# Making the last tile ahead of a norm in two halves of the tokens

## The chip, the cores and the metric

The kernel runs on one core of a Trainium2 chip. Its engines work side by side, each through its own queue in order: TensorE (PE; its weight loads are listed as PEld), VectorE (DVE), ScalarE (ACT), GpSimd (POOL) and SyncE (SP), which issues transfers. The metric is the device time of one execution in microseconds, the median over several runs.

## The reference

Two layers of a transformer-like trunk over 256 context tokens and 256 image tokens of width 1024. The context is needed as keys and values only in layer 1, so layer 0 works on 512 tokens and layer 1, after its keys and values, on 256. What matters here is how each half of a layer ends:

```python
def rms_norm(x, w):
    xf = x.astype(jnp.float32)
    y = xf * lax.rsqrt(jnp.mean(xf * xf, axis=-1, keepdims=True) + RMS_EPS)
    return (y * w.astype(jnp.float32)).astype(x.dtype)
...
    x = x + g1 * parallel_mixers(p, attn, lp)        # ends in merged @ w_out
    x = x + g2 * swiglu(modulate(x, norm2_w[l], sh2, s2), ffn_w_gate[l], ffn_w_up[l], ffn_w_down[l])
return rms_norm(x, final_norm_w)
```

A norm needs the sum of squares over all 1024 features of a token, so nothing after it can start until the last feature tile of `x` is there.

## The kernel before

Activations lie with features on the 128 partitions and tokens on the free axis: `x` is 8 tiles of 128 x 512, of which layer 1 uses the right 256 columns. Float32 products are made of three fp32r products: each operand is split into a high part and a rest (`whi`, `wlo`, `hh`, `hl`), and `mm3` (lines 209 to 211) issues high x high, high x rest and rest x high into one PSUM accumulation.

Weights arrive as units of 128 x 1024 in `raw`; ScalarE casts them to `whi` (line 171), VectorE subtracts to get `wlo` (line 174). There are five buffers for `raw` and four each for `whi` and `wlo`, so the cast of a unit waits until the unit four before it is used up.

Four places in the program have the same shape: 8 output tiles `j` are made one after another, each of 24 products (w_out, k = 0..7) or 33 (w_dn, second half of the FFN, k = 0..10), and the last one is followed by a norm.

- A: w_out of layer 0, then norm 2, then the first FFN products (`k_major`, PSUM tiles `pmk`)
- B: w_dn of layer 0, then norm 1 of layer 1, then `wide_gen` (`pmw`)
- C: w_out of layer 1, then norm 2 and `k_major`
- D: w_dn of layer 1, then the final norm and the output

After each tile `residual` adds it to `x` on VectorE; `sumsq_add` squares `x[j]` on ScalarE and adds the square to `acc` on VectorE. Around the last tile `sums_of` multiplies `acc`, and then the last square, with a column of ones on TensorE (PSUM tile `pmss`): the sums over the partitions, one column for every 128 tokens. `rstd` scales and adds epsilon on VectorE (`rs`) and takes the power -1/2 on GpSimd. `rstd_bcast` makes a diagonal matrix of it on VectorE (`dg`) and multiplies it with ones on TensorE, which gives the factor on all partitions (`psrb`). `norm_tiles` then makes `nt`, `nh`, `hh` and `hl` of the 8 tiles on VectorE and ScalarE.

While this chain runs, TensorE is given other work: filters of the next layer (`pspf`), spectra (`pssp`), and modulation matmuls (`psmod`, `chunk_mods`). At the end (D), `x` is weighted (`xw`, ScalarE), transposed on TensorE into `psfin`, scaled by the factor into `fin`, and written out by four transfers of 256 KB.

The order on each engine comes from the order of the code and a scheduler that moves instructions by its own estimate; `tc.keep_in_program_order` holds an instruction at its place. On the chip each queue is in order: an instruction that waits holds all that stand behind it.

Of the kernel before, what the change touches and what calls it, by code (L numbers as in the profile page):

```python
# [14 lines left out]
AF = mybir.ActivationFunctionType  # L15
# [3 lines left out]
P = 128  # L19
D = 1024  # L20
# [82 lines left out]
def trunk_kernel(ctx: ExitStack, tc: tile.TileContext, I, out: bass.AP):  # L103
# [32 lines left out]
    def load_const(name, shape):  # L136
        t = const(name, shape)
        SY.dma_start(out=t, in_=I[name])
        return t

    def split(hi, lo, src):
        S.copy(hi, src)
        V.tensor_sub(lo, src, f32(hi))
# [63 lines left out]

    def mm3(o, wh, wl, xh, xl, first, last):
        T.matmul(o, lhsT=wh, rhs=xh, start=first, stop=False)  # L209
        T.matmul(o, lhsT=wh, rhs=xl, start=False, stop=False)  # L210
        T.matmul(o, lhsT=wl, rhs=xh, start=False, stop=last)  # L211

# [14 lines left out]
    ones = const("ones", [P, P])  # L227
    V.memset(ones, 1.0)
    halfexp = const("halfexp", [P, 8])
    V.memset(halfexp, -0.5)  # L230
# [51 lines left out]
    def chunk_mods(n):  # L282
        for _ in range(min(n, len(chunks))):
            c, kt, raw = chunks.popleft()
            if kt == 0:
                mod_bank[c] = side("mod")
            o = mod_bank[c]
            for q in range(4):
                T.matmul(
                    o[32 * q : 32 * q + 32, :P], lhsT=csf[:, kt, :], rhs=raw[:, q * P : q * P + P],  # L290
                    start=(kt == 0), stop=(kt == KT - 1),
                )
            if kt == KT - 1:
                chunk_tail(c)
# [28 lines left out]

    def last_sq(x, c0, c1):
        sq = t2(s="sq")
        S.activation(sq[:, c0:c1], x[KT - 1][:, c0:c1], AF.Square)
        return sq

    def sums_of(o, v, c0, c1, first, last):

        nt = (c1 - c0) // P
        for t in range(nt):
            sl = slice(c0 + t * P, c0 + t * P + P)
            T.matmul(
                o[:, t : t + 1], lhsT=v[:, sl], rhs=ones[:, 0:1],
                start=first and t == 0, stop=last and t == nt - 1,
            )
# [10 lines left out]
    def rstd_bcast(r2, c0, c1):  # L348

        nt = (c1 - c0) // P  # L350
# [7 lines left out]
        )  # L358
        rb = side("rb")
        T.matmul(rb[:, c0:c1], lhsT=ones, rhs=dg[:, : c1 - c0], start=True, stop=True)  # L360
        return rb

# [97 lines left out]
    def filter_mm(l, p, o):  # L460
        w3, _, f = flt[l]
        f[p, o] = side("pf")
        T.matmul(f[p, o], lhsT=hk[:, p * P : p * P + P], rhs=w3[o], start=True, stop=True)

# [184 lines left out]
    r2 = rstd(o, 0, NTOK)  # L649
    rb = rstd_bcast(r2, 0, NTOK)  # L650
    chunk_mods(KT)
# [3 lines left out]
    for l in range(DEPTH):  # L655
# [28 lines left out]
        if l == 0:  # L684
# [5 lines left out]
            for g in range(4):  # L690
# [11 lines left out]
                os_ = next(w0)  # L702
            start.close()
        else:
            for i, h in enumerate(norm_tiles(l, 0, x, rb, 0, NTOK, range(KT))):
# [533 lines left out]
        def residual(o, j, gi):  # L1239
            for k in halves:  # L1240
# [3 lines left out]
                )  # L1244

        if l == 0:
# [3 lines left out]
        for j in range(KT):  # L1250
# [4 lines left out]
            if j == KT - 1:  # L1255
                so = bank("ss")
                sums_of(so, acc, C0, NTOK, True, False)
                if full:
                    filter_mm(1, 0, 0)
            residual(o, j, 2)  # L1260
            if j < KT - 1:
                sumsq_add(x, acc, j, C0, NTOK)
# [4 lines left out]
        sums_of(so, last_sq(x, C0, NTOK), C0, NTOK, False, True)  # L1267
        r2 = rstd(so, C0, NTOK)
# [4 lines left out]
        if full:  # L1273
            filter_mm(1, 1, 0)
        chunk_mods(BUB[1])

# [4 lines left out]
        if full:  # L1281
            for po in ((0, 0), (0, 1), (1, 0)):
                filter_keep(1, *po)
            filter_mm(1, 1, 1)
            filter_keep(1, 1, 1)
        acc = t2(s="acc")
        xw, fin = {}, {}

        def final_weigh(j):
            xw[j] = t2(s="xw")  # L1290
            S.activation(xw[j][:, CS], x[j][:, CS], AF.Copy, scale=nw[:, 2 * DEPTH, j : j + 1])

        def final_turn(j):

            for t in range(NX // P):
                if j % 4 == 0:
# [4 lines left out]
        for half in range(2):  # L1301
# [18 lines left out]
            for j in range(KT):  # L1320
                o = bank("d")
                for k in range(NFH):
                    n = j * NFH + k
                    if n % 8 == 0:
                        hi, lo = unit("w_dn", l, half, n // 8)
                    c = (n % 8) * P
                    mm3(
                        o[:, CS], hi[:, c : c + P], lo[:, c : c + P],
                        hid[k][0][:, CS], hid[k][1][:, CS], k == 0, k == NFH - 1,
                    )  # L1330
                    if n % 8 == 7:
                        done()
                if half == 1 and j == KT - 1:
                    for _ in sg_:
                        pass
                    so = bank("ss")
                    sums_of(so, acc, C0, NTOK, True, False)
                    if full:
                        parts, fwd, nyq, skip = flt[1]
                        spectrum_mm(1, "B0", parts, fwd, nyq)  # L1340
                residual(o, j, 5)
                if half == 1 and j < KT - 1:
                    sumsq_add(x, acc, j, C0, NTOK)
                if not full and half == 1:
                    if j:
                        final_turn(j - 1)
                    if j < KT - 1:
                        final_weigh(j)
                next(sg_, None)
        sums_of(so, last_sq(x, C0, NTOK), C0, NTOK, False, True)  # L1350
        r2 = rstd(so, C0, NTOK)
        if full:
            spectrum_out(1, "B0", skip)
            spectrum_mm(1, "B1", parts, fwd, nyq)
            spectrum_out(1, "B1", skip)
            spectrum_mm(1, "A0", parts, fwd, nyq)
            rb = rstd_bcast(r2, C0, NTOK)
            spectrum_mm(1, "A1", parts, fwd, nyq)
            spectrum_mm(1, "C0", parts, fwd, nyq)


    final_weigh(KT - 1)
    final_turn(KT - 1)
    for t in range(NX // P):
        for h in range(2):
            y = t2(s="fin")
            if h:
                S.activation(y, fin[t, h], AF.Copy, scale=r2[:, t : t + 1])
            else:
                V.tensor_scalar(y, fin[t, h], r2[:, t : t + 1], None, op0=ALU.mult)  # L1370
            SY.dma_start(out=out[t * P : t * P + P, h * 512 : h * 512 + 512], in_=y)

# [154 lines left out]
```

## Time and profile before

| | us |
|---|---|
| median of 3 runs (1328.41 to 1329.69) | 1329.41 |
| profiled execution | 1328.54 |
| its span, first to last instruction | 1326.0 |
| TensorE busy (matmul) | 1292.9 |
| VectorE busy | 935.6 |
| ScalarE busy | 608.6 |

A timeline row gives the start in us from the span's start, the duration in us, the engine, the source line, the operation, out<-in tiles, their shape (for a matmul 128*128 is the weight and 128x512 the moving operand), and how many were merged; in brackets how long the engine had been idle, and what released it. A matmul's duration is a latency: in a row of products the distance of two starts is what one costs.

### The profile page before, as it was taken

The page shows a single profiled execution, that of the slowest core. Times are in us where ns is not written, and L with a number is a line of the kernel's source. Part 1 is how long each engine was busy: PE and PEld are TensorE (multiplying, and loading weights), DVE is VectorE, ACT ScalarE, POOL GpSimd, SP SyncE. Part 2 cuts the span into 40 slices and gives each one's busy share as a digit, 9 for nine tenths or more (in the row PEclk, how much of TensorE's full clock was granted, in tenths as well). Part 3 has the DMA queues.
Part 4 walks back from the last instruction along what each step waited for, and adds up shares of the span by engine and source line. Part 5 has one row for each costly group of instructions (what it writes and reads, how often), then busy time and mean ns, then how long its engine had stood idle before and what let it go on. Part 6 is the DMA issues. An engine that isn't in the chain of part 4 may idle for free.

```text
span 1326.0 us, 19996 instructions
## 1 busy us (share of the span) xinstructions
PE 1292.9 (98%) x7714; PEld 1128.2 (85%) x7714; DVE 935.6 (71%) x1599; ACT 608.6 (46%) x1060; POOL 61.9 (5%) x69
## 2 busy tenths in 40 slices
PE   4999999999999999999999999999999999999997
PEld 3778788888888887888888888889989999999997
DVE  3687788798987356666667767966889876655554
ACT  3564333367753246222222224365468854543443
POOL 0000500300000000000000000001210000000000
PEclk7999999999999999999999999999999999999999
DMA  9532334343245552554555554424434457455551
GB/s 343 210 127 77 104 104 143 126 143 112 93 157 160 174 209 73 173 164 159 174 174 175 182 168 143 159 80 128 134 110 139 151 192 247 159 179 188 179 187 49
DMA packets 68063, 203.85 MB, mean 154 GB/s; under 512 B 7552, under 2 KB 13824, under 8 KB 67968
## 3 DMA queue, kind: packets, MB, share of 16 engines
q1 hardware_dynamic: 67968, 202.58, 46.1%
q8 instruction: 60, 0.98, 0.3%
q14 instruction: 35, 0.29, 0.1%
HBM read 201.50 MB, written 1.05 MB: 153 GB/s over the span
## 4 chain that ended last, share of the span: by engine, by line
PE 75%; issue 16%; DVE 5%; ACT 2%; POOL 1%; DMA 0%; DVEq 0%; POOLq 0%; ACTq 0%
PE pmn L209 14%; PE pmn L211 14%; PE pmn L210 14%; PE pmd L209 3%; PE pmd L210 3%; PE pmd L211 3%; PE pmb L209 2%; PE pmb L210 2%; PE pmb L211 2%; PE pmw L676 2%; PE pmw L678 2%; PE pmw L677 2%; PE psav L1188 1%; PE pspt L1166 1%; DVE wlo L174 1%
## 5 line engine op out<-in xcount | busy, mean ns | idle before, releaser
L171 ACT CAST whi<-raw 128x1024 fp32r<-128x1024 f32 (+2 forms) x312 | 288.1, 929 | 470.8 <-PE pmn L210 214.4
L209 PE MATMUL pmn<-hh,whi 128*128 128x512 f32 (+1 forms) x1328 | 449.9, 339 | 0.3 <-DVE vst L721 0.3
L210 PE MATMUL pmn<-hl,whi 128*128 128x512 f32 (+1 forms) x1328 | 448.1, 337 | 0.0
L211 PE MATMUL pmn<-hh,wlo 128*128 128x512 f32 (+1 forms) x1328 | 447.7, 337 | 0.3 <-DVE wlo L174 0.3
L174 DVE TENSOR_TENSOR wlo<-raw,whi 128x1024 fp32r<-128x1024 f32 (+2 forms) x312 | 335.7, 1078 | 143.3 <-ACT whi L171 141.0
L211 PEld LDWEIGHTS pmn<-hh,wlo 128*128 128x128 f32 x1328 | 252.0, 190 | 27.7 <-issue 1.1
L209 PEld LDWEIGHTS pmn<-hh,whi 128*128 128x128 f32 x1328 | 252.1, 190 | 27.6 <-issue 0.9
L210 PEld LDWEIGHTS pmn<-hl,whi 128*128 128x128 f32 x1328 | 252.1, 190 | 26.0 <-issue 0.7
L259 DVE CUSTOM_DVE_ANT_0 junk<-raw,cb,pack_a 128x1024 bf16<-128x1024 f32 x144 | 187.0, 1299 | 1.4
L209 PE MATMUL pmd<-hh,whi 128*128 128x512 f32 (+1 forms) x352 | 119.2, 339 | 0.0
L210 PE MATMUL pmd<-hl,whi 128*128 128x512 f32 (+1 forms) x352 | 118.7, 337 | 0.0
L211 PE MATMUL pmd<-hh,wlo 128*128 128x512 f32 (+1 forms) x352 | 118.0, 336 | 0.0
L210 PEld LDWEIGHTS pmd<-hl,whi 128*128 128x128 f32 x352 | 66.8, 190 | 7.2 <-issue 0.5
L211 PEld LDWEIGHTS pmd<-hh,wlo 128*128 128x128 f32 x352 | 66.8, 190 | 7.1 <-issue 0.2
L209 PEld LDWEIGHTS pmd<-hh,whi 128*128 128x128 f32 x352 | 66.8, 190 | 7.1 <-issue 0.2
L1314 DVE TENSOR_TENSOR sg<-sg,pmn 128x512 f32<-128x512 f32 (+1 forms) x42 | 23.3, 554 | 65.0 <-PE pmn L211 65.0
L345 POOL TENSOR_TENSOR rs<-rs,halfexp 128x4 f32<-128x4 f32 (+1 forms) x5 | 4.4, 884 | 956.9 <-DVE rs L343 956.9
L676 PE MATMUL pmw<-whi,hh 128*128 128x512 f32 (+1 forms) x112 | 43.8, 392 | 3.8 <-ACT hh L389 3.8
L677 PE MATMUL pmw<-wlo,hh 128*128 128x512 f32 (+1 forms) x112 | 42.5, 380 | 0.0
L678 PE MATMUL pmw<-whi,hl 128*128 128x512 f32 (+1 forms) x112 | 42.4, 382 | 0.0
L387 ACT ACTIVATE nh<-nt,mod,amod 128x256 f32<-128x256 f32 x51 | 28.0, 594 | 24.4 <-DVE nt L377 19.2
L1242 DVE SCALAR_TENSOR_TENSOR x<-pmd,mod,x 128x256 f32<-128x256 f32 x48 | 21.8, 476 | 24.5 <-PE pmd L211 24.5
(275 smaller groups left out, 1872.7 us busy)
## 6 DMA issues: line engine op xcount, KB each, us to landing
raw<-in_w_ff SPq DMA_DIRECT2D x88, 512.0 KB, 4.3
raw<-in_w_nar SPq DMA_DIRECT2D x84, 512.0 KB, 3.5
raw<-in_w_t SPq DMA_DIRECT2D x72, 512.0 KB, 3.6
raw<-in_w_dn SPq DMA_DIRECT2D x44, 512.0 KB, 4.2
raw<-in_w_mod SPq DMA_DIRECT2D x48, 256.0 KB, 6.0
raw<-in_w_wide SPq DMA_DIRECT2D x16, 512.0 KB, 3.6
raw<-in_w_out SPq DMA_DIRECT2D x16, 512.0 KB, 3.9
raw<-in_w_br SPq DMA_DIRECT2D x48, 128.0 KB, 2.2
```

The source lines that it names most:

```text
L171: S.copy(hi[:, :n], raw[:, :n])
L174: V.tensor_sub(lo[:, :n], raw[:, :n], f32(hi[:, :n]))
L209: T.matmul(o, lhsT=wh, rhs=xh, start=first, stop=False)
L210: T.matmul(o, lhsT=wh, rhs=xl, start=False, stop=False)
L211: T.matmul(o, lhsT=wl, rhs=xh, start=False, stop=last)
L259: r = V.tensor_tensor_reduce(out=junk, in0=raw, in1=cb[:, s, :], scale=1.0, scalar=bmod[:, l, i : i + 1], op0=ALU.mult, op1=ALU.add, accum ...
L387: S.activation(h[:, a0:a1], t[:, a0:a1], AF.Identity, bias=sh, scale=a[:, j, k : k + 1])
L676: T.matmul(os_[t][:, :n], lhsT=hh[:, sl], rhs=wh, start=(kt == 0), stop=False)
L677: T.matmul(os_[t][:, :n], lhsT=hh[:, sl], rhs=wl, start=False, stop=False)
L678: T.matmul(os_[t][:, :n], lhsT=hl[:, sl], rhs=wh, start=False, stop=(kt == 7))
L1242: V.scalar_tensor_tensor(x[j][:, sl], o[:, sl], mod[l][:, gi * 8 + j, k : k + 1], x[j][:, sl], op0=ALU.mult, op1=ALU.add)
L1314: V.tensor_mul(sg[:, CS], sg[:, CS], o[:, CS])
```

## The change

In each of the four places the last tile is made by the new `last_tile`: first all products for the left half of the tokens, then all for the right half, each half in a PSUM bank of its own. A half is 256 columns in layer 0 and 128 in layer 1. The sums of `acc` stand within or behind the first half's products, and the first half's square, sums, `rstd` and diagonal stand beside the second half's products. The second half has a chain of its own. Both broadcasts follow (`rstd_spread`), with the other work of TensorE dealt out in three `fills`. At D nothing is broadcast: each half is scaled and written out by its own factor, and two of the four transfers are issued by ScalarE. The sums multiply with a column `part` of 1/1024, so `rstd` only adds epsilon. `pin` holds the sums, broadcasts, modulation and layer 1's filter matmuls at their place in the code (after the opening).

```diff
     def sums_of(o, v, c0, c1, first, last):
...
-            T.matmul(
-                o[:, t : t + 1], lhsT=v[:, sl], rhs=ones[:, 0:1],
-                start=first and t == 0, stop=last and t == nt - 1,
-            )
+            pin(T.matmul(
+                o[:, t : t + 1], lhsT=v[:, sl], rhs=part, start=first and t == 0, stop=last and t == nt - 1,
+            ))
...
-        V.tensor_scalar(r[:, :nt], o[:, :nt], 1.0 / D, EPS, op0=ALU.mult, op1=ALU.add)
+        V.tensor_scalar(r[:, :nt], o[:, :nt], EPS, None, op0=ALU.add)
...
+        spans = [(0, 256, 0), (256, 512, 1)] if full else [(256, 384, 1), (384, 512, 1)]
+
+        def last_tile(steps, gi, acc, spread, fills, also=None):
+
+            j = KT - 1
+            so = [bank("ss") for _ in spans]
+            rs = []
+
+            def sums(n):
+                c0, c1, _ = spans[n]
+                sums_of(so[n], sqs[n], c0, c1, False, True)
+                rs.append(rstd(so[n], c0, c1))
+                return rstd_diag(rs[n], c0, c1) if spread else None
+
+            sqs, dgs = [], []
+            for n, (c0, c1, k) in enumerate(spans):
+                sl = slice(c0, c1)
+                o = bank("h")
+                for i, (wh, wl, (xh, xl)) in enumerate(steps):
+                    if i == len(steps) // 2:
+                        if n:
+                            dgs.append(sums(0))
+                            if also:
+                                also(0)
+                        else:
+                            for m, (a0, a1, _) in enumerate(spans):
+                                sums_of(so[m], acc, a0, a1, True, False)
+                    mm3(o[:, sl], wh, wl, xh[:, sl], xl[:, sl], i == 0, i == len(steps) - 1)
+                V.scalar_tensor_tensor(
+                    x[j][:, sl], o[:, sl], mod[l][:, gi * 8 + j, k : k + 1], x[j][:, sl], op0=ALU.mult, op1=ALU.add
+                )
+                sq = t2(s="sq")
+                S.activation(sq[:, sl], x[j][:, sl], AF.Square)
+                sqs.append(sq)
+                if also:
+                    final_weigh(j, sl)
+            fills[0]()
+            dgs.append(sums(1))
+            fills[1]()
+            if spread:
+                rb = side("rb")
+                for dg, (c0, c1, _) in zip(dgs, spans):
+                    rstd_spread(rb, dg, c0, c1)
+            fills[2]()
+            return rb if spread else rs
...
         if full:
-            filter_mm(1, 0, 1)
-        chunk_mods(BUB[0])
-        rb = rstd_bcast(r2, C0, NTOK)
-        if full:
-            filter_mm(1, 1, 0)
-        chunk_mods(BUB[1])
+            fills = (
+                fill_((filter_mm, 1, 0, 0), (filter_keep, 1, 0, 0)),
+                fill_((filter_mm, 1, 0, 1), (filter_keep, 1, 0, 1), (filter_mm, 1, 1, 0)),
+                fill_((chunk_mods, 4)),
+            )
+        else:
+            fills = fill_((chunk_mods, 2)), fill_((chunk_mods, 4)), fill_((chunk_mods, 2))
+        rb = last_tile([(hi[:, k * P : k * P + P], lo[:, k * P : k * P + P], merged[k]) for k in range(KT)], 2, acc, True, fills)
+        done()
...
+            def also(n):
+                if n == 0:
+                    final_turn(KT - 2)
+                final_turn(KT - 1, [n])
+
+            rs = last_tile(steps, 5, acc, False, [fill_(), fill_((also, 1)), fill_()], also)
+            for t in range(NX // P):
+                for h in range(2):
...
+                    (S if h else SY).dma_start(out=out[t * P : t * P + P, h * 512 : h * 512 + 512], in_=y)
```

Three places in the order show what moves. The first is TensorE at place C, before: the end of the last tile (`pmn_10818`), modulation matmuls and the sums of `acc` and of the last square.

```order
L209 MATMUL pmn_10818<-mgh_10554,whi_10773 128x256
L210 MATMUL pmn_10818<-mgl_10555,whi_10773 128x256
L211 MATMUL pmn_10818<-mgh_10554,wlo_10774 128x256
L289 MATMUL psmod_10861<-raw_10732,csf 32x128 x4
L289 MATMUL psmod_10861<-raw_10734,csf 32x128 x4
L289 MATMUL psmod_10861<-raw_10736,csf 32x128 x4
L289 MATMUL psmod_10861<-raw_10738,csf 32x128
L334 MATMUL pmss_10849<-ones,acc_10558 128x1 x2
```

And TensorE at the same place in the changed kernel, within the first half (`pmh_10901`).

```order
L216 MATMUL pmh_10901<-mgh_10492,whi_10854 128x128
L217 MATMUL pmh_10901<-mgl_10493,whi_10854 128x128
L218 MATMUL pmh_10901<-mgh_10492,wlo_10855 128x128
L216 MATMUL pmh_10901<-mgh_10550,whi_10854 128x128
L342 MATMUL pmss_10899<-part,acc_10639 128x1
L342 MATMUL pmss_10900<-part,acc_10639 128x1
L217 MATMUL pmh_10901<-mgl_10551,whi_10854 128x128
L218 MATMUL pmh_10901<-mgh_10550,wlo_10855 128x128
```

The sums of `acc` moved from behind the tile to behind the sixteenth of the first half's 24 products; 32 products of the tile now stand behind them.

The second is VectorE at place C, before: residuals of tiles 6 and 7 (`x_4365`, `x_4367`), the additions to `acc`, a weight's rest and the norm's `rs` and diagonal.

```order
L1242 SCALAR_TENSOR_TENSOR x_4365<-pmn_10783,mod_89,x_4365 128x256
L174 TENSOR_TENSOR wlo_10887<-raw_10812,whi_10886 128x1024
L322 TENSOR_TENSOR acc_10558<-acc_10558,sq_10780 128x256
L1242 SCALAR_TENSOR_TENSOR x_4367<-pmn_10818,mod_89,x_4367 128x256
L322 TENSOR_TENSOR acc_10558<-acc_10558,sq_10815 128x256
L174 TENSOR_TENSOR wlo_11041<-raw_10847,whi_11040 128x1024
L343 TENSOR_SCALAR rs_10857<-pmss_10849 128x2
L353 TENSOR_TENSOR dg_10878<-pack_a,rs_10859 128x256
L381 SCALAR_TENSOR_TENSOR nt_10895<-x_4353,amod_93,psrb_10880 128x256
```

The same stretch of VectorE in the changed kernel, where `x_4367` is tile 6 and `x_4369` tile 7.

```order
L180 TENSOR_TENSOR wlo_11019<-raw_10893,whi_11018 128x1024
L335 TENSOR_TENSOR acc_10639<-acc_10639,sq_10861 128x256
L335 TENSOR_TENSOR acc_10639<-acc_10639,sq_10896 128x256
L1286 SCALAR_TENSOR_TENSOR x_4369<-pmh_10901,mod_91,x_4369 128x128
L350 TENSOR_SCALAR rs_10945<-pmss_10899 128x1
L359 TENSOR_TENSOR dg_10949<-pack_a,rs_10947 128x128
L1286 SCALAR_TENSOR_TENSOR x_4369<-pmh_10931,mod_91,x_4369 128x128
L180 TENSOR_TENSOR wlo_11158<-raw_11016,whi_11157 128x1024
L350 TENSOR_SCALAR rs_10976<-pmss_10900 128x1
L359 TENSOR_TENSOR dg_10980<-pack_a,rs_10978 128x128
L313 STREAM_TRANSPOSE modt_11009<-psmod_10966 128x128
L389 SCALAR_TENSOR_TENSOR nt_11027<-x_4355,amod_95,psrb_10998 128x256
```

The first half's chain went ahead of the second residual; a weight's rest still stands between that residual and the second `rs`, and the transpose of the modulation moved ahead of the first `nt`.

The third is ScalarE at place C in the changed kernel: squares of tiles 5 and 6, the two squares of tile 7's halves, and a weight cast.

```order
L334 ACTIVATE sq_10861<-x_4365 128x256
L334 ACTIVATE sq_10896<-x_4367 128x256
L1290 ACTIVATE sq_10929<-x_4369 128x128
L177 CAST whi_11157<-raw_11016 128x1024
L1290 ACTIVATE sq_10964<-x_4369 128x128
L392 ACTIVATE hh_11029<-nt_11027,mod_91 128x256
```

The cast, which stood between the squares of tiles 6 and 7, stands between the squares of the two halves of tile 7.

## Rows read from the trace of the kernel before

**Rows 1.** The page's first part: span, TensorE's busy time, share, instructions.

```profile
span 1326.0 us, 19996 instructions
...
PE 1292.9 (98%) x7714; PEld 1128.2 (85%) x7714; DVE 935.6 (71%) x1599; ACT 608.6 (46%) x1060; POOL 61.9 (5%) x69
```

**Rows 2.** Waits of TensorE: who waited for whom, total us, times, longest.

```profile
PE psrb L360 <- DVE dg L353: 4.3, 4, 2.1
...
PE pmk L209 <- ACT hh L384: 1.6, 2, 1.1
```

**Rows 3.** Timeline at place A (layer 0, last tile of w_out).

```profile
488.08 0.39 PE L209 MATMUL pmn<-mgh,whi 128*128 128x512 f32 x1
...
490.29 0.68 DVE L322 TENSOR_TENSOR acc<-acc,sq 128x512 f32<-128x512 f32 x1
...
493.30 0.39 PE L211 MATMUL pmn<-mgh,wlo 128*128 128x512 f32 x1
...
501.78 0.96 PE L209 MATMUL pmk<-hh,whi 128*128 128x512 f32 x3 [0.51 <-ACT hh L384]
```

**Rows 4.** Timeline at place B (layer 0, behind the last tile of w_dn).

```profile
865.92 0.39 PE L211 MATMUL pmd<-hh,wlo 128*128 128x512 f32 x1
...
871.91 1.13 PE L360 MATMUL psrb<-dg,ones 128*128 128x512 f32 x2 [0.80 <-DVE dg L353]
...
875.41 0.19 PEld L676 LDWEIGHTS pmw<-whi,hh 128*128 128x128 f32 x1
```

**Rows 5.** Timeline at place C (layer 1, last tile of w_out, norm 2).

```profile
1115.72 0.28 PE L209 MATMUL pmn<-mgh,whi 128*128 128x256 f32 x1
...
1118.07 0.42 DVE L322 TENSOR_TENSOR acc<-acc,sq 128x256 f32<-128x256 f32 x1
...
1118.48 0.28 PE L211 MATMUL pmn<-mgh,wlo 128*128 128x256 f32 x1
...
1118.73 1.04 ACT L171 CAST whi<-raw 128x1024 fp32r<-128x1024 f32 x1 [1.20 <-issue]
...
1119.80 1.22 DVE L174 TENSOR_TENSOR wlo<-raw,whi 128x1024 fp32r<-128x1024 f32 x1 [0.19 <-ACT whi L171]
...
1121.22 0.16 DVE L343 TENSOR_SCALAR rs<-pmss 128x2 f32<-128x2 f32 x1 [0.19 <-PE pmss L334]
...
1124.55 0.62 PE L209 MATMUL pmk<-hh,whi 128*128 128x256 f32 x3 [1.11 <-ACT hh L384]
...
1127.80 0.31 DVE L300 STREAM_TRANSPOSE modt<-psmod 128x128 f32<-128x128 f32 x1
```

**Rows 6.** Timeline at place D (layer 1, last tile of w_dn, output).

```profile
1313.48 0.36 PE L209 MATMUL pmd<-hh,whi 128*128 128x256 f32 x1
...
1317.40 0.28 PE L211 MATMUL pmd<-hh,wlo 128*128 128x256 f32 x1
...
1321.10 1.82 SPq L1371 DMA_DIRECT2D out<-fin  x4
```

**Rows 7.** Timeline of TensorE's weight loads: transposes, sums of squares, plain f32.

```profile
1009.67 0.46 PEld L1166 LDWEIGHTS pspt<-pack_a,pe 128*128 128x128 f32 x4
1010.10 0.19 PEld L1188 LDWEIGHTS psav<-pth,vst 128*128 128x128 f32 x1
...
865.92 1.08 PEld L334 LDWEIGHTS pmss<-ones,acc 128*128 128x128 f32 x8
866.92 0.19 PEld L210 LDWEIGHTS pssp<-fl,dh 128*128 128x128 f32 x1
...
495.28 0.19 PEld L463 LDWEIGHTS pspf<-w,hyh 128*128 128x128 f32 x1 [0.24 <-issue]
495.71 0.19 PEld L334 LDWEIGHTS pmss<-ones,sq 128*128 128x128 f32 x1 [0.24 <-issue]
```

**Rows 8.** Stretches of 2 us in place C: busy us, instructions, granted clock, DMA.

```profile
1126.00:1128.00 2.00, 2.00 (x11) 2.00 (x11) 1.47 (x5) 1.97 (x6) 0.00 (x0) 0.50 0.05 18
...
1130.00:1132.00 2.00, 2.00 (x19) 2.00 (x18) 0.76 (x2) 1.09 (x3) 0.00 (x0) 1.00 0.01 4
```

More of the change, by code (lines that the diff above doesn't have):

```diff
@@ L139, in load_const, with pin @@
         return t
+    def pin(r):
+        if not opening:
+            tc.keep_in_program_order(r)
+    opening = [True]
     def split(hi, lo, src):
@@ L206, in done, with mm3 @@
         flush()
[L208 to L211, printed above, removed]
+    def mm3(o, wh, wl, xh, xl, first, last, held=False):
+        rs = [
+            T.matmul(o, lhsT=wh, rhs=xh, start=first, stop=False),
+            T.matmul(o, lhsT=wh, rhs=xl, start=False, stop=False),
+            T.matmul(o, lhsT=wl, rhs=xh, start=False, stop=last),
+        ]
+        if held:
+            for r in rs:
+                pin(r)
     pa = load_const("pack_a", [P, 280])
@@ L358, in rstd_bcast, with rstd_spread @@
         )
-        rb = side("rb")
-        T.matmul(rb[:, c0:c1], lhsT=ones, rhs=dg[:, : c1 - c0], start=True, stop=True)
-        return rb
+        return dg
+    def rstd_spread(rb, dg, c0, c1):
+        pin(T.matmul(rb[:, c0:c1], lhsT=ones, rhs=dg[:, : c1 - c0], start=True, stop=True))
     def norm_tiles(l, which, x, rb, c0, c1, js, between=None):
@@ L462, in filter_mm @@
         f[p, o] = side("pf")
[L463 removed]
+        r = T.matmul(f[p, o], lhsT=hk[:, p * P : p * P + P], rhs=w3[o], start=True, stop=True)
+        if l:
+            pin(r)
     def filter_keep(l, p, o):
@@ L703, in trunk_kernel @@
             start.close()
+            opening.clear()
         else:
@@ L1249, in trunk_kernel @@
         os_, _ = k_major([("w_out", l, j) for j in range(3)], merged, CS)
-        for j in range(KT):
+        for j in range(KT - 1):
             if j < 3:
@@ L1287, in trunk_kernel, with final_weigh, final_turn @@
         xw, fin = {}, {}
[L1289 to L1295, printed above, removed]
+        def final_weigh(j, sl=CS):
+            if j not in xw:
+                xw[j] = t2(s="xw")
+            S.activation(xw[j][:, sl], x[j][:, sl], AF.Copy, scale=nw[:, 2 * DEPTH, j : j + 1])
+        def final_turn(j, ts=range(NX // P)):
+            for t in ts:
                 if j % 4 == 0:
@@ L1320, in trunk_kernel @@
             for j in range(KT):
-                o = bank("d")
+                steps = []
+                tail = half == 1 and j == KT - 1
+                o = None if tail else bank("d")
                 for k in range(NFH):
@@ L1326, in trunk_kernel @@
                     c = (n % 8) * P
+                    if tail:
+                        steps.append((hi[:, c : c + P], lo[:, c : c + P], hid[k]))
+                        continue
                     mm3(
@@ L1332, in trunk_kernel @@
                         done()
[L1333 to L1340, printed above, removed]
+                if tail:
+                    break
                 residual(o, j, 5)
-                if half == 1 and j < KT - 1:
+                if half == 1:
                     sumsq_add(x, acc, j, C0, NTOK)
@@ L1346, in trunk_kernel @@
                         final_turn(j - 1)
-                    if j < KT - 1:
-                        final_weigh(j)
+                    final_weigh(j)
                 next(sg_, None)
-        sums_of(so, last_sq(x, C0, NTOK), C0, NTOK, False, True)
-        r2 = rstd(so, C0, NTOK)
+        for _ in sg_:
+            pass
         if full:
[L1353 to L1371, printed above, removed]
+            parts, fwd, nyq, skip = flt[1]
+            fills = (
+                fill_((spectrum_mm, 1, "B0", parts, fwd, nyq), (spectrum_out, 1, "B0", skip)),
+                fill_((spectrum_mm, 1, "B1", parts, fwd, nyq), (spectrum_out, 1, "B1", skip)),
+                fill_(*[(spectrum_mm, 1, n, parts, fwd, nyq) for n in ("A0", "A1", "C0")]),
+            )
+            rb = last_tile(steps, 5, acc, True, fills)
+            done()
+        else:
+            def also(n):
[5 more added lines that the diff above has]
+                for h in range(2):
+                    y = t2(s="fin")
+                    if h:
+                        S.activation(y, fin[t, h], AF.Copy, scale=rs[t][:, 0:1])
+                    else:
+                        V.tensor_scalar(y, fin[t, h], rs[t][:, 0:1], None, op0=ALU.mult)
+                    (S if h else SY).dma_start(out=out[t * P : t * P + P, h * 512 : h * 512 + 512], in_=y)
 def _constants():
```

34 lines of the change are left out of this document (15 added, 19 removed).

## Prediction

> **What bounds the kernel now.** I read the page's first part, then the waits of TensorE, then the timeline around the four places that the change touches. TensorE is busy for 98% of the span [rows 1], so a change counts by what it adds to TensorE's stream and by the waits that it takes out of it. The waits that end in a norm's chain are small: all waits for the broadcast matmul `psrb` come to 4.3 us at four places, one of them (2.1 us) in the opening, and those for the first normalised tile `hh` come to 1.6 us at two [rows 2]. That is the pool from which three of the four places can win. The fourth is the end of the program, where the last product starts at 1317.40 and the span goes on to 1326.0 [rows 1, 6].
>
> **The price of a product.** The change splits each last tile by tokens: 24 products (w_out) or 33 (w_dn) of N columns become 48 or 66 of N/2. In layer 0 N is 512: products start every 0.227 us (488.08 to 493.30, 23 steps) [rows 3]. Halves have 256 columns, which layer 1 shows: every 0.120 us (1115.72 to 1118.48, 23 steps) [rows 5]. So layer 0 pays 48 x 0.120 - 24 x 0.227 = +0.3 us and 66 x 0.120 - 33 x 0.227 = +0.4 us.
>
> In layer 1 N is 256 and halves have 128 columns; no such fp32r product is in the trace. Call its price S. From below: 0.227 and 0.120 differ by 0.107 for 256 columns, so columns alone give 0.120 - 0.053 = 0.067 us. From above: a plain f32 matmul of 512 columns is two records 0.43 us apart [rows 7], 0.86 us, or 0.215 for 128 columns. The nearest rows are instructions that also load a full 128x128 f32 weight and stream 128 columns or fewer. Four transposes with 128 columns take 0.43 us (1009.67 to 1010.10), 0.107 each; eight records of the sums of squares, with a single column, take 1.00 us (865.92 to 866.92), 0.125 each [rows 7]. The second shows that the load alone holds TensorE for some 0.11 to 0.13 us, however few columns follow. I take S = 0.12: in layer 1 a half costs what the whole did, and the tile doubles.
>
> [...]
>
> **Place A, w_out to norm 2, layer 0.** The tile starts at 488.08. In the new stream 48 products take 5.8 us, the eight records of the accumulated sums 1.0 and the four of the first half's square 0.5; the last product starts near 495.2, where 493.30 stood. The sums don't stall, as `acc` is done at 490.97 [rows 3] and 24 half products end at 490.96. Behind the last product the way to `pmk` took 8.48 us [rows 3]; it sheds the sums that came forward and a wider diagonal, and I work it out at about 6.4. Net -0.1 us. Bounds: no more can be won than TensorE waited here, a share of [rows 2], so -1.5; and +0.8 if the cast ahead of the second square delays it by most of a microsecond (the order on ScalarE is as at place C).
>
> **Place B, w_dn to norm 1 of layer 1.** The last product moves from 865.92 to about 868.0 by the same count (66 x 0.120 + 1.0 + 0.5). The 0.80 us for which TensorE stood at `psrb` (871.91) goes, since spectrum products are ordered between the two halves' broadcasts; the fill that stood ahead of the first `pmw` load at 875.41 [rows 4] is the same work. Net -0.4 us, between -1.0 and +0.4.
>
> **Place C, w_out to norm 2, layer 1.** 24 x 0.12 = 2.88 us become 48S = 5.76. The sums of `acc` now stand after 16 products inside the first half, and TensorE's queue is in order, so all the products behind them wait. They need tile 6 in `acc`. VectorE adds tile 5 at 1118.07 for 0.42 us and the order puts tile 6 right behind: ready at 1118.9 [rows 5]. The first sixteen products and the start-up of the seventeenth take 17S = 2.0 us from 1115.72: TensorE waits 3.18 - 17S = 1.1 us. Four records for `acc` and two for the first square add 0.75. So the last product comes 2.88 + 1.1 + 0.75 = 4.7 us later.
>
> Does the chain behind it get shorter? Before: from 1118.48 to the reciprocal root's input `rs` at 1121.22 is 2.74 us, and to `pmk` 6.07 [rows 5]. In it a weight cast on ScalarE (1118.73, 1.04 us) precedes the last square and its rest `wlo` on VectorE (1119.80, 1.22 us) precedes `rs`. Both stay in the same places in the order, and the cast writes into the buffer that the last tile's weights hold until its second half ends. So the second half's square still waits behind the cast and its `rs` behind `wlo`. Smaller instructions win a few tenths; a STREAM_TRANSPOSE that ran at 1127.80 for 0.31 us [rows 5] moves ahead of the first `nt` and takes them back. I take 0 for the chain: +4.7 us for C. Bounds of the chain: -2.3 if cast and `wlo` fall out of it wholly, +0.8 if the transpose waits for the modulation matmuls that come after `psrb`.
>
> **Place D, the end.** The last tile starts at 1313.48, and the last of 33 products at 1317.40 [rows 6]. Now: 66S = 7.9 us, four records of `acc` and two of the first square (0.75), three transposes of the first half (3 x 0.107). `acc` is no late comer here: ScalarE and VectorE have no weight casts left in this tile. The last product starts at 1322.4, +5.0 us. Behind it: before, 3.70 us to the first output DMA, 1.82 for four issues, and 3.08 to the end of the span (1321.10 + 1.82 to 1326.0). Now one token tile is out before; the other's instructions are half as wide (3.70 to about 3.15), two issues remain on ScalarE and one on SyncE (0.85), and half of the bytes (3.08 to about 2.4): 6.4 instead of 8.6, -2.2, give or take 0.6. Nothing waits behind the DMAs that go to ScalarE's queue. D: +2.8 us.
>
> **No cost of their own.** `part` instead of a column of `ones` and the scale that `rstd` drops change no instruction count on the path. Four more powers on GpSimd lie beside products. The pinned order moves four modulation groups from before `pmk` into the loop behind it at A and one filter product the other way, about 0.9 us each; I count them as even.
>
> **The sum.** As a function of S below 0.187: A and B -0.5, C 31S + 1.05, D 66S - 5.08, together 97S - 4.5. With 0.12: +7 us. The profiled execution had 1328.54 us (span 1326.0 and 2.5 around it), 0.9 below the median 1329.41 of the runs. So 1335.5 in its terms and **1336.4** as a median: 0.5% slower. A measurement of this kernel can tell 0.2%, or 2.7 us, from no change.
>
> **Rivals.**
> - *The column count sets the price* (0.067; the weight load hides). For it: the clean line from 512 to 256 columns. Against it: the one-column records at 0.125. C is then +3.1 (the wait for `acc` grows to 2.0), D -0.7, the sum +2.0: 1331.4, no change that can be measured. It decides from S = 0.074 down; faster needs the low ends of the chains at A, B and C besides. Chance 0.14.
> - *A narrow fp32r product runs at the plain f32 rate* (0.215). For it: nothing in the trace excludes it, and plain f32 rows exist. Against it: fp32r keeps the same price per column at 512 and 256. The wait at C is gone then, the formula is 114S - 7.7, the sum +16.8: 1346. Chance 0.12.
> - *The clock falls inside the narrow stream.* [...] Half-empty products might bring that on. If half of the 114 go at double price: 57 x 0.12 = +6.8 more, 1343. [...] Chance 0.10.
> - My forecast keeps 0.64; with S from 0.107 to 0.125 and the chains' bounds its own range is 1332.5 to 1338.5.
>
> **Range and chances.** 1331 to 1346 leaves out the lower part of the first rival and the tail of the second. Faster by over 0.2%: 0.05 (first rival with short chains). Within 0.2%: 0.13 (the rest of that rival, and the forecast with its chains at the low ends). Slower: 0.82.
>
> **What would show it.** In the profile after: `pmh` products of 128 columns starting every 0.12 us (0.067 or 0.215 for the rivals); a wait of `pmss` for `acc` of about 1 us at C; first `pmk` of layer 1 some 4.7 us later after its tile's start; the first cast behind the last tile starting only when the second half ends; 6.4 us from the last `pmh` to the end of the span; A and B within half a microsecond of before. I am wrong if 128-column products start in under 0.08 us, or if the second half's chain at C and D is over 2 us shorter than I have it.

## The result and the profile after

| kernel | median us | lowest to highest | runs |
|---|---|---|---|
| before | 1329.41 | 1328.41 to 1330.00 | 5 |
| after | 1340.31 | 1339.82 to 1342.04 | 5 |

The ratio is 1.0088, 95% interval 1.0074 to 1.0102: the change costs 10.9 us. The profiled execution of after is the slowest of its five, 1342.04 us with a span of 1340.2 (the median run's span is 1338.5), so its trace shows 14.2 us more span than before's [rows 1], and some 3 of them lie where nothing was changed. The page's first part:

```profile
span 1340.2 us, 20259 instructions
...
PE 1308.0 (98%) x7834; PEld 1142.2 (85%) x7834; DVE 937.3 (70%) x1609; ACT 609.5 (45%) x1065; POOL 65.7 (5%) x73
```

TensorE has 15.1 us more busy time than in [rows 1], in 120 more instructions, and stands idle for 32.2 us of the span, 33.1 before. Its waits (who for whom, total us, times, longest):

```profile
PE pmss L342 <- DVE acc L335: 8.8, 2, 7.3
...
PE psrb L369 <- DVE dg L359: 2.1, 1, 2.1
PE pmss L342 <- ACT sq L1290: 1.5, 3, 0.8
```

Against [rows 2] the waits at `psrb` outside the opening are gone, 2.2 us in all. In their place stand 1.5 us for `acc` (the 7.3 belong to the opening) and 1.5 us for the square of the half that ended.

To see where the time goes, I took the start of the same TensorE instruction in both timelines, ahead of and behind each place. The growth of the difference over a place is what the place costs (us):

| | ahead of A | A | A to C, with B | C | D | sum |
|---|---|---|---|---|---|---|
| forecast | 0 | -0.1 | -0.4 | +4.7 | +2.8 | +7.0 |
| trace of after | +2.8 | +1.3 | +0.2 | +7.5 | +2.4 | +14.2 |

**Place A.** The tile's first product, its last, and what follows on TensorE:

```profile
490.84 0.28 PE L216 MATMUL pmh<-mgh,whi 128*128 128x256 f32 x1
...
498.03 0.28 PE L218 MATMUL pmh<-mgh,wlo 128*128 128x256 f32 x1
...
499.65 0.61 PE L342 MATMUL pmss<-part,sq 128*128 128x1 f32 x4 [0.47 <-ACT sq L1290]
...
502.87 1.08 PE L302 MATMUL psmod<-raw,csf 128*32 128x128 f32 x32
504.46 0.98 PE L216 MATMUL pmk<-hh,whi 128*128 128x512 f32 x3 [0.51 <-ACT hh L392]
...
512.38 0.39 PE L218 MATMUL pmk<-hh,wlo 128*128 128x512 f32 x1
512.70 0.43 PE L302 MATMUL psmod<-raw,csf 128*32 128x128 f32 x8
...
513.39 0.39 PE L217 MATMUL pmk<-hl,whi 128*128 128x512 f32 x1
```

From first product to `pmk` 13.62 us, where [rows 3] have 13.70: the forecast's chain is right. But only 32 `psmod` records lie ahead of `pmk`, where there were 64; four groups of 8 now lie between the `pmk` products. Such a group costs 0.56 us there: from 512.38 to 513.39 two steps take 1.01 us, and 0.45 us where no group stands between. Four groups make 2.2 us. In return one filter product (two records) moved ahead of `pmk`. It stood among the `pmk` products before and cost 0.88 us there: three steps in 1.56 us, from 507.19 to 508.75, instead of 0.68.

```profile
507.42 1.02 PE L463 MATMUL pspf<-w,hyh 128*128 128x512 f32 x2
```

With the 0.08 us of the chain that is 2.2 - 0.9 - 0.1, about the +1.3 of the table.

**Place C.** TensorE around the first half's sums and at the end of the tile:

```profile
1121.69 0.28 PE L216 MATMUL pmh<-mgh,whi 128*128 128x128 f32 x1
1123.41 0.61 PE L342 MATMUL pmss<-part,acc 128*128 128x1 f32 x4 [1.44 <-DVE acc L335]
...
1128.42 0.41 PE L217 MATMUL pmh<-mgl,whi 128*128 128x128 f32 x1
1128.64 0.41 PE L218 MATMUL pmh<-mgh,wlo 128*128 128x128 f32 x1
...
1132.61 1.22 PE L369 MATMUL psrb<-dg,ones 128*128 128x128 f32 x4
1133.76 1.08 PE L302 MATMUL psmod<-raw,csf 128*32 128x128 f32 x16
1136.19 1.01 PE L216 MATMUL pmk<-hh,whi 128*128 128x256 f32 x3 [1.34 <-ACT hh L392]
```

The wait is 1.44 us. The last eleven products start every 0.214 us. The stretches (the number ahead of the last two is the granted clock) show why:

```profile
1124.00:1126.00 2.00, 2.00 (x20) 2.00 (x20) 0.35 (x1) 0.31 (x1) 0.00 (x0) 1.00 1.04 413
1126.00:1128.00 2.00, 2.00 (x14) 2.00 (x13) 0.45 (x2) 0.00 (x0) 0.55 (x1) 0.61 1.01 406
...
1138.00:1140.00 2.00, 2.00 (x12) 2.00 (x11) 1.47 (x5) 1.97 (x6) 0.00 (x0) 0.50 0.00 0
1140.00:1142.00 2.00, 2.00 (x18) 2.00 (x18) 1.54 (x5) 2.00 (x5) 0.00 (x0) 0.98 0.00 0
```

From 1126.4 to 1140.1 the granted clock is 0.50. VectorE behind the tile:

```profile
1130.00 1.22 DVE L180 TENSOR_TENSOR wlo<-raw,whi 128x1024 fp32r<-128x1024 f32 x1 [0.56 <-ACT whi L177]
1131.14 0.15 DVE L350 TENSOR_SCALAR rs<-pmss 128x1 f32<-128x1 f32 x1
...
1134.91 0.32 DVE L313 STREAM_TRANSPOSE modt<-psmod 128x128 f32<-128x128 f32 x1 [2.66 <-PE psmod L302]
1135.15 0.44 DVE L389 SCALAR_TENSOR_TENSOR nt<-x,amod,psrb 128x256 f32<-128x256 f32 x1
```

The transpose ahead of the first `nt` waits for the 16 `psmod` records that TensorE runs behind `psrb`: from `psrb` to `pmk` 3.6 us, 1.8 before (1122.76, and 1124.55 in [rows 5]). The lower clock has a part in this: the 16 records last 1.08 us here, and 0.64 us at a clock of 1.00 in the run below that has the sums later.

**Place D.** First product, the first and last of twelve that follow one another without other work between, and last product:

```profile
1325.29 0.30 PE L216 MATMUL pmh<-hh,whi 128*128 128x128 f32 x1
...
1325.66 0.28 PE L216 MATMUL pmh<-hh,whi 128*128 128x128 f32 x1
...
1326.89 0.27 PE L218 MATMUL pmh<-hh,wlo 128*128 128x128 f32 x1
...
1333.53 0.28 PE L218 MATMUL pmh<-hh,wlo 128*128 128x128 f32 x1
```

Eleven steps take 1.23 us, 0.112 each. The last product comes 8.24 us behind the first (3.92 in [rows 6]), and 6.67 us ahead of the end of the span (8.60).

### The profile page after: what moved, and what is told of

It is laid out like the page before. It is cut to its first block, busy times and chain, and to the rows that moved or that the text cites. A ratio compares the mean times of both kernels' runs of the same rounds, so it can differ in the third digit from the quotient of the medians.

```text
span 1340.2 us, 20259 instructions
## 1 busy us (share of the span) xinstructions
PE 1308.0 (98%) x7834; PEld 1142.2 (85%) x7834; DVE 937.3 (70%) x1609; ACT 609.5 (45%) x1065; POOL 65.7 (5%) x73
## 4 chain that ended last, share of the span: by engine, by line
PE 87%; DVE 6%; ACT 2%; DMA 2%; issue 1%; POOL 1%; SPq 0%; POOLq 0%; ACTq 0%; DVEq 0%
PE pmn L216 17%; PE pmn L218 17%; PE pmn L217 17%; PE pmd L217 4%; PE pmd L216 4%; PE pmd L218 4%; PE pmb L216 2%; PE pmb L217 2%; PE pmb L218 2%; DVE wlo L180 1%; PE pmw L687 1%; PE psav L1200 1%; PE pmk L216 1%; PE pmw L689 1%; PE pmw L688 1%
## 5 line engine op out<-in xcount | busy, mean ns | idle before, releaser
L216 PE MATMUL pmd<-hh,whi 128*128 128x512 f32 (+1 forms) x330 | 111.7, 339 | 0.0
L217 PE MATMUL pmd<-hl,whi 128*128 128x512 f32 (+1 forms) x330 | 111.3, 337 | 0.0
L218 PE MATMUL pmd<-hh,wlo 128*128 128x512 f32 (+1 forms) x330 | 110.7, 336 | 0.0
L217 PEld LDWEIGHTS pmd<-hl,whi 128*128 128x128 f32 x330 | 62.7, 190 | 6.8 <-issue 0.5
L218 PEld LDWEIGHTS pmd<-hh,wlo 128*128 128x128 f32 x330 | 62.6, 190 | 6.7 <-issue 0.2
L216 PEld LDWEIGHTS pmd<-hh,whi 128*128 128x128 f32 x330 | 62.6, 190 | 6.7 <-issue 0.2
L352 POOL TENSOR_TENSOR rs<-rs,halfexp 128x2 f32<-128x2 f32 (+2 forms) x9 | 6.9, 767 | 968.3 <-DVE rs L350 968.3
L1163 ACT ACTIVATE pe<-pssc,mx 128x512 f32<-128x512 f32 (+1 forms) x48 | 29.6, 617 | 16.5 <-DVE mx L1160 16.4
```

Source lines behind the costliest of these rows:

```text
L216: T.matmul(o, lhsT=wh, rhs=xh, start=first, stop=False),
L217: T.matmul(o, lhsT=wh, rhs=xl, start=False, stop=False),
L218: T.matmul(o, lhsT=wl, rhs=xh, start=False, stop=last),
L1163: S.activation(e[:, :nk], sc[:, :nk], AF.Exp, bias=mx, scale=1.0, accum_out=den)
```

## Experiments

The forecast was 4 us short. My theory: half-width products cost what was forecast (0.112 us), and the rest is two side effects, the modulation groups at A and the clock at C, which falls because TensorE stands for `acc`. The main rival: the narrow stream itself brings the clock down. In the edits `HALF` names the tiles made in halves, as (layer, 2 for w_out or 5 for w_dn); the others have the code of before. The costs by place of all runs stand in the table at the end of this section.

**One layer or place alone.**

```diff
-HALF = {(0, 2), (0, 5), (1, 2), (1, 5)}
+HALF = {(0, 2), (0, 5)}    # e1_layer0
+HALF = {(1, 2)}            # e2_placeC
+HALF = {(1, 5)}            # e3_placeD
```

> Only the last tiles of layer 0 (places A and B) are made in halves; layer 1 as before. Theory (the trace after): A costs +1.35 us from its first product to a product that both kernels share behind it, because four groups of modulation matmuls that ran in TensorE's waits ahead of the first pmk now run between the pmk products; from A to B +0.2, B 0.0. Sum +1.6: 1331.0 us. Rival (the terms of the forecast: A -0.1, B -0.4, moved groups even): 1328.9 us. If the 1 us that the profile after lost ahead of the first pmw came from the change (the column `part`), both are 1.0 higher, and the first pmw starts at about 31.0 us instead of 30.1.

> Only w_out's last tile of layer 1 (place C) is made in halves. Theory: TensorE stands 1.4 us for acc, its granted clock falls to 0.50 some 2 us after that and stays there until about 14 us later; the last pmh comes 8.6 us behind the first, the first pmk 16.1 us behind it (8.83 before), the sum +7.5: 1336.9 us. Rival (forecast, a clock of 1.00 until TensorE waits for hh): +4.7, 1334.1 us.

> Only w_dn's last tile of layer 1 (place D) is made in halves. Theory: 66 products at 0.112 us without a wait, clock 1.00, last product 8.2 us behind the first (3.92 before), 6.7 us from it to the end of the span (8.6 before): +2.4, 1331.8 us. Rival (narrow products bring the clock down by themselves): the clock falls here too, half of the products at double price, +6: 1335.4 us.

Layer 0 alone: ratio 1.0013 (1.0004 to 1.0022), +1.7 us, the theory's number, and all of it at A (+1.4). C alone: 1.0068 (1.0055 to 1.0081), +9.0 us, more than either number; its runs spread from 1335.3 to 1339.4. D alone: 1.0014 (1.0005 to 1.0023), +1.9 us, clock 1.00 through 66 narrow products: this stream, with no stand in it, did not bring the clock down. In C alone the clock fell at 1120.6, 0.8 us behind the wait's end instead of 3.0 as in after, and was back only at 1137.7, so 29 products ran at 0.214 instead of 11:

```profile
1119.81 0.61 PE L343 MATMUL pmss<-part,acc 128*128 128x1 f32 x4 [1.44 <-DVE acc L336]
...
1120.88 0.41 PE L219 MATMUL pmh<-mgh,wlo 128*128 128x128 f32 x1
```

**The sums of `acc` later.**

```diff
+if l == 1 and gi == 2 and n == 1 and i == 3:   # was: n == 0 and i == len(steps) // 2
     for m, (a0, a1, _) in enumerate(spans):
         sums_of(so[m], acc, a0, a1, True, False)
```

> The change whole, but at place C the sums of acc stand after 33 of the 48 products instead of after 16, when acc is done, so that TensorE does not stand for it. Theory (the wait brings the clock down): no wait, clock 1.00 to the last product, 48 products in 6.0 us, the chain behind it 6.1 instead of 7.55 us; 4.0 us less than after, 1336.3 us. Rival (the narrow stream brings the clock down): the clock falls to 0.50 all the same, only the wait is saved, 1338.9 us.

Measured 1335.6 us, ratio 1.0045 (1.0033 to 1.0058). No wait, and the clock is 1.00 past the last product, which comes 5.87 us behind the first. The sums' row, the tile's last product and the first `pmk`, and the sums' stretch of 2 us:

```profile
1122.16 0.55 PE L343 MATMUL pmss<-part,acc 128*128 128x1 f32 x4
...
1124.39 0.27 PE L219 MATMUL pmh<-mgh,wlo 128*128 128x128 f32 x1
...
1130.43 0.62 PE L217 MATMUL pmk<-hh,whi 128*128 128x256 f32 x3 [1.34 <-ACT hh L398]
```

```profile
1122.00:1124.00 2.00, 2.00 (x20) 2.00 (x20) 0.24 (x2) 0.31 (x1) 0.45 (x1) 1.00 1.08 399
```

The same narrow stream at the same place keeps its clock when TensorE doesn't stand in it. C goes from +7.5 to +3.1. From the last product to `pmk` are 6.04 us, though the transpose waits as in after: 6.1 was expected, 6.07 stood there before, and after took 7.55. So the 1.5 us that the chain lost in after belong to the lower clock.

**All three side effects mended** (the sums later, as above, and these).

```diff
-fills = fill_((chunk_mods, 2)), fill_((chunk_mods, 4)), fill_((chunk_mods, 2))   # layer 1
+fills = fill_((chunk_mods, 2)), fill_((chunk_mods, 6)), fill_()
-fill_((filter_mm, 1, 0, 0), (filter_keep, 1, 0, 0)),                             # layer 0
+fill_((filter_mm, 1, 0, 0), (filter_keep, 1, 0, 0), (chunk_mods, 2)),
-fill_((chunk_mods, 4)),
+fill_((chunk_mods, 5)),
```

> The change whole with its three side effects mended: at C the sums of acc after 33 products (as in the run before) and all eight groups of modulation matmuls ahead of psrb, so that the transpose ahead of the first nt need not wait for the last two; at A three of the four groups that the change moved between the pmk products stand ahead of the first pmk again. Theory: A +0.4 instead of +1.4 (its waits of 0.5 us in front of pmss and of pmk take the groups), C +2.5 instead of +3.1, D +2.4, together +5.4 over before (1328.7): 1334.1 us. What is left is the price of the narrow products in layer 1. Rival (the moved modulation matmuls are even, as the forecast had it): 1335.6 us as in the run before.

Measured 1332.91 us, under the theory's 1334.1; ratio 1.0033 (1.0021 to 1.0044), +4.4 us. From the last product to `pmk` at C are 5.23 us, 0.8 less than with the transpose waiting. A is -0.4, C +0.8 (the trace of before has a clock fall of its own at C, which this one lacks; see the table). What is left is the narrow products of layer 1, C and D.

**A wait in a whole tile, and its control.** The control only puts C's tile through the new function as one span; the other adds the late copy. In the control's order the sums of `acc` come behind the whole tile, with the late copy behind its fifteenth product.

```diff
-spans = [(256, 384, 1), (384, 512, 1)]
+spans = [(256, 512, 1)]                          # both, place C
+V.scalar_tensor_tensor(xs[:, CS], acc[:, CS], 0.0, f32(xh[:, CS]), op0=ALU.mult, op1=ALU.add)
+steps[5] = wh, wl, (xs, xl)                      # e6_wait_whole alone
```

> Place C without narrow products: the last w_out tile of layer 1 is one tile of 256 columns, as before, but TensorE is made to stand in it: the sums of acc come after 15 of its 24 products, and the two products behind them read a copy of their operand that VectorE makes out of acc (0.48 us more on VectorE). All else as before, the modulation matmuls pinned as in the change. Theory (the wait alone brings the clock down): TensorE stands some 1.8 us, the granted clock falls to 0.50 within 3 us behind that and stays there past the first pmk; C is 3.5 to 5 us longer than before, 1332 to 1333.5 us. Rival (it takes narrow products as well): the clock stays 1.00 up to the wait for hh, C is 2.4 us longer, 1331.1 us.

> The control to the wait in a whole tile: the last w_out tile of layer 1 whole, no wait put into it, the modulation matmuls pinned as in the change (two groups ahead of the sums, four behind them, two behind psrb, whose transpose stands ahead of the first nt). Theory: the clock stays 1.00 until TensorE waits for hh; the transpose waits for the two groups, C +0.6: 1329.3 us. Rival (the pinned order by itself brings the clock down): C +2 or more.

With the wait: ratio 1.0024 (1.0015 to 1.0033); control: 1.0004 (0.9995 to 1.0013). The wait's row, the stretches behind it, and the control's stretches behind its last product (1121.63):

```profile
1122.01 0.61 PE L343 MATMUL pmss<-part,acc 128*128 128x1 f32 x4 [1.39 <-DVE acc L336]
```

```profile
1122.00:1124.00 2.00, 2.00 (x12) 2.00 (x13) 0.41 (x1) 0.00 (x0) 0.00 (x0) 0.68 1.05 410
1124.00:1126.00 2.00, 1.73 (x20) 1.02 (x19) 0.98 (x2) 1.36 (x2) 0.00 (x0) 0.50 1.03 414
1126.00:1128.00 2.00, 1.58 (x36) 1.30 (x36) 1.19 (x3) 0.00 (x0) 0.70 (x1) 0.96 0.66 211
```

```profile
1122.00:1124.00 2.00, 1.67 (x32) 1.38 (x28) 1.81 (x3) 1.24 (x2) 0.00 (x0) 1.00 1.07 410
1124.00:1126.00 2.00, 1.28 (x34) 0.93 (x26) 0.67 (x3) 0.00 (x0) 0.69 (x1) 1.00 1.02 408
```

In this execution the clock fell behind the wait, without one narrow product. But the cost, 2.75 us over the control at C, is below the theory's 3.5 to 5: here the clock was back some 3.5 us after it fell, where after stayed down for 14 and C alone for 17. The median, 1332.51 us, lies in the theory's range. Four of the ten runs take 1331.1 to 1331.3 us, which is the rival's time, and whether the clock fell in those no trace shows.

Such a wait is not always followed by a fall. All twelve traces have one of 1.47 to 1.51 us at 165 to 167 us, far ahead of the four places. In four of them (after, D alone, the whole tile with a wait and its control) the clock fell within 1 us of its end; in the other eight it stayed at 1.00. The wait and a stretch behind it, in before and then in after:

```profile
165.38 0.49 PE L209 MATMUL psiv<-yh,dft_ih 128*128 128x512 f32 x1 [1.47 <-ACT yh L142]
...
168.00:170.00 2.00, 2.00 (x10) 1.65 (x10) 1.39 (x5) 0.53 (x1) 0.81 (x1) 1.00 0.37 90
```

```profile
166.56 0.50 PE L216 MATMUL psiv<-yh,dft_ih 128*128 128x512 f32 x1 [1.50 <-ACT yh L148]
...
168.00:170.00 2.00, 2.00 (x6) 1.54 (x5) 2.00 (x7) 0.45 (x2) 0.48 (x1) 0.50 0.00 0
```

So the wait is what the fall at C came behind, but the length of a wait alone does not settle whether one comes. The next run asks what kept the clock down.

**A wait in the narrow stream of place D.**

```diff
+for _ in range(4):                               # place D, first half, step 3
+    V.scalar_tensor_tensor(ys[:, CS], acc[:, CS], 0.0, f32(xs[:, CS]), op0=ALU.mult, op1=ALU.add)
+    xs = ys
+late[3] = wh, wl, (xs, xl)
```

> Only place D in halves, and TensorE is made to stand in the narrow stream: two products of the first half read a copy that VectorE makes out of acc in four steps (some 2 us). What keeps the clock down for 14 to 17 us at place C, where a fall elsewhere lasts some 3.5? Theory (narrow products, once the clock is down, don't bring it back): the clock falls behind the wait and stays at 0.50 to the end of the stream, some 55 products at 0.21 us; D +10 over before, 1339 us. Rival (the clock comes back after some 3.5 us whatever runs): some 16 products at 0.21, D +6, 1335 us. Without a fall it would be +4.6, 1333.6 us.

Ratio 1.0073 (1.0059 to 1.0086), 9.2 us at D in the trace against 2.4 without the wait. The wait and the last product of the tile, then stretches behind the wait:

```profile
1317.43 0.33 PE L217 MATMUL pmh<-xs,whi 128*128 128x128 f32 x1 [1.46 <-DVE xs L1289]
...
1328.81 0.41 PE L219 MATMUL pmh<-hh,wlo 128*128 128x128 f32 x1
```

```profile
1318.00:1320.00 2.00, 2.00 (x19) 2.00 (x18) 0.00 (x0) 0.00 (x0) 0.00 (x0) 0.92 0.05 8
1320.00:1322.00 2.00, 2.00 (x11) 2.00 (x11) 0.31 (x1) 0.00 (x0) 0.00 (x0) 0.50 0.00 0
...
1326.00:1328.00 2.00, 2.00 (x12) 2.00 (x11) 0.00 (x0) 0.00 (x0) 0.00 (x0) 0.50 0.00 0
```

The clock fell at 1319.7 and did not return in 9 us of narrow products, although TensorE counts as busy in all of that time. At D in after the same products ran for 8 us at 1.00. At C in after only the first 2.3 us behind the fall were narrow products; the clock stayed down through the modulation matmuls and waits behind them too, and came back 3.9 us after the products of 256 columns had begun at 1136.19. In the whole tile with a wait it came back behind products of 256 columns and modulation matmuls. No run puts whole products behind a wait at D, so it is not shown that the width alone made the difference.

**Two smaller ones: the output queue, and layer 0 mended.**

```diff
-SY.dma_start(out=out[...], in_=y)                 # e7_two_queues: before with this edit alone
+(S if h else SY).dma_start(out=out[...], in_=y)
```

> The kernel before with one edit: two of the four output DMAs are issued on ScalarE's queue, two on SyncE's. No tile in halves. Theory: two issues instead of four stand behind one another (0.9 instead of 1.82 us); from the last product to the end of the span 7.7 us instead of 8.6; 1327.8 us. Of the 1.9 us that the end won at place D, this part needs no narrow products. Rival (the output's bytes set the end): 8.6 us, 1328.7.

> Only layer 0 in halves, with three of the four groups of modulation matmuls back ahead of the first pmk at place A. Theory: A -0.4 us (as the mended kernel's trace had it), B 0: 1328.6 us against 1329.0 before, not to be told from it by the time, but to be read at place A: first pmh to first pmk about 13.6 us, with 56 instead of 32 psmod records ahead of the first pmk. Rival (the moved groups had no part): A +1.4, 1330.4 us as with layer 0 alone.

Two queues: ratio 0.9999 (0.9991 to 1.0008). The issues are shorter, but the span does not end earlier: 1317.75 to 1326.5 is 8.75 us from the last product, 8.60 before.

```profile
1321.40 0.92 ACTq L1476 DMA_DIRECT2D out<-fin  x2
1321.46 1.00 SPq L1476 DMA_DIRECT2D out<-fin  x2
```

So the second queue by itself does not give the end's gain at D. What is left is that half of the output is out early and that the instructions are narrower; no run separates the two. Layer 0 mended (HALF of the first run, the layer 0 edits of the mended kernel): 1327.64 against 1328.60, ratio 0.9992 (0.9983 to 1.0001); 56 `psmod` records ahead of `pmk`, A -0.4, B 0. It is the only version with halves that is not slower than before, and its interval does not exclude no change.

```profile
497.34 0.64 PE L303 MATMUL psmod<-raw,csf 128*32 128x128 f32 x16
...
501.14 1.30 PE L303 MATMUL psmod<-raw,csf 128*32 128x128 f32 x40
502.72 0.97 PE L217 MATMUL pmk<-hh,whi 128*128 128x512 f32 x3 [0.28 <-ACT hh L398]
```

Cost by place against the trace of before (us); an asterisk marks a place that the kernel leaves as in before:

| kernel | A | B | C | D |
|---|---|---|---|---|
| after | +1.3 | 0.0 | +7.5 | +2.4 |
| e1_layer0 | +1.4 | 0.0 | +0.1* | 0.0* |
| e2_placeC | 0.0* | 0.0* | +9.1 | 0.0* |
| e3_placeD | 0.0* | 0.0* | -1.4* | +2.5 |
| e4_late | +1.4 | 0.0 | +3.1 | +2.4 |
| e5_mended | -0.4 | +0.4 | +0.8 | +2.4 |
| e6_wait_whole | 0.0* | +0.4* | +1.8 | +0.1* |
| e8_whole_pinned | 0.0* | 0.0* | -0.9 | 0.0* |
| e7_two_queues | 0.0* | +0.4* | -1.2* | +0.1 |
| e9_layer0_mended | -0.4 | 0.0 | -1.2* | +0.1* |
| e10_wait_D | 0.0* | +0.2* | -1.4* | +9.2 |

C varies by 1.4 us where it is unchanged: before [rows 8] and e1_layer0 have a clock fall behind C, the four at -1.2 to -1.4 have none. Like with like: the kernel with the sums late has such a fall, +3.1 against before; the mended one has none, +2.1 against those four.

## Why the prediction was right, and where it fell short

The direction was right and the range (1331 to 1346) held 1340.31, but the forecast, 1336.4, was 3.9 us short, and its own range (1332.5 to 1338.5) did not hold the time. That the wide range held it is partly luck: its upper end came from a price of 0.215 for the narrow product, which did not come true, and not from what happened at C.

- **S**, the price of a half-width product: taken as 0.12, measured 0.112 (1325.66 to 1326.89, 11 steps) at a clock of 1.00. Both rivals on S, 0.067 and 0.215, fall; the 0.214 at C is the lower clock. The bound that I drew from one-column records (0.125 each) was near the price. That the weight load alone sets it was my estimate from those records and the transposes (0.107); it is not shown, as no run has the narrow product without a new load.
- **A**, -0.1, measured +1.3. The chain was right to 0.1 us. What failed is "I count them as even", with "about 0.9 us each". The filter product that went the other way was worth 0.88 us, but the four modulation groups cost 2.2 us: they moved from the waits ahead of `pmk`, where they cost nothing (13.70 us from the tile's first product to `pmk` with 64 records there, 13.62 with 32), to where TensorE is full. With three of them put back, A is -0.4 (layer 0 mended).
- **B**, -0.4, measured 0.0. The 0.80 us at `psrb` went, as said, but the first `pmw` came as late as before: longer stream and shorter wait cancel.
- **C**, +4.7, measured +7.5. The wait for `acc` was forecast (1.1 us, measured 1.44), and so were the cast and `wlo` ahead of `rs` (2.50 us from the last product to `rs`; 2.74 before). What failed is the clock of 1.00 in the sum. Eleven products at 0.214 instead of 0.112 cost 1.1 us and the chain at the lower clock 1.5, together 2.6 of the 2.8 us that C is over the forecast. I gave a fall 0.10, as something that half-empty products might bring on. Its double price came from the granted clock of 0.50 in [rows 8], and 0.214 against 0.112 was measured. The wait at C was in the forecast as 1.1 us and no more. That wait is what the fall came behind: with the sums put later there is none in the tile, and with a wait put in there is one in a whole tile and at D. The rival had the effect and not its cause. "0 for the chain" holds at a clock of 1.00 (6.04 us with the sums later, 6.07 before), as two things that cancel: the transpose does wait for the modulation matmuls behind `psrb`, the bound of +0.8, and without that wait the chain is 0.8 us shorter than before. With both mended C costs 2.1, like with like.
- **D**, +2.8, measured +2.4: the stream +4.3 (+5.0 forecast, of which S at 0.112 takes off 0.5), the end -1.9 (-2.2). I had booked shorter issues on two queues as a gain; alone they bring none (8.75 us from the last product to the end of the span, 8.60 before).
- **Ahead of A** the trace of after is 2.8 us late: 1.2 up to the wait at 165 to 167 us, most of it in the opening, and 1.6 in a clock fall at 167 to 171. The opening varies: the wait of `pmw` for `hh` ends at 31.00 here, at 30.09 in before and between 29.2 and 31.3 in all twelve traces. The fall stands in four of the twelve, and the other three are of kernels that have the code of before up to C or D. So both belong to the execution.

Why three of the four places win nothing when the waits really go: the waits were 2.2 us in all outside the opening, and new ones of about that size came in their place.

What stays open: why a wait of 1.4 to 1.5 us is followed by a fall in some executions and not in others, and what brings the clock back. Behind the opening the runs show only what stood before it rose: products of 256 or 512 columns, in places with modulation matmuls behind them.

## What to carry to other kernels

Before splitting a matmul's moving operand, ask what a product costs at the new width: in these runs halves are free at 512 columns (0.227 to 2 x 0.120 us) and double the tile at 256 (0.120 to 2 x 0.112). When work is moved for the sake of a chain, ask what sat in the waits that go: filler that ran for nothing there costs its time elsewhere, here 0.56 us a group. And before putting a consumer of another engine's result into the middle of a dense TensorE stream, check when that result is ready: a stand of 1.4 us cost 4.4 us at C and 6.8 at D, the stand itself included, and most of it by the clock.

## What the runs showed of the hardware

- Behind a stand of 1.39 to 1.46 us in a full stream at C or D the granted clock fell to 0.50, between 0.7 and 3.0 us after TensorE had resumed (four of four traces). Behind the wait of 1.47 to 1.51 us at 165 to 167 us it fell in four of twelve traces, and behind the wait of 1.11 to 1.34 us for `hh` at C in three of the ten in which it was up.
- Once down, it did not come back in 9 us of fp32r products of 128 columns (0.50 from 1319.7 to the last product at 1328.81, with the wait at D), although a clock of 1.00 held through 8 us of the same products at D in after. Where products of 256 columns followed (behind C in before, and in the whole tile with a wait), it was back some 3.5 us after it fell.
- The same code falls in some executions only: behind C before runs at 0.50 [rows 8]; the kernel with two output queues, the same there, has this row.

```profile
1126.00:1128.00 2.00, 1.68 (x13) 1.65 (x14) 1.83 (x7) 1.70 (x5) 0.00 (x0) 1.00 0.53 213
```

Falls like these are worth 1.2 to 1.6 us each, and the runs of before lie within 3.3 us of one another (1327.0 to 1330.3 in 28).
